# An encoder on one core: first column blocks side by side, a shared sine product, and the order of high and low weight products

## Chip, cores and metric

The kernel runs on one core of a Trainium2 chip. The metric is the device time of one execution in microseconds (us); lower is better. Each time is compared with runs of the kernel before on the same chip.

## The reference

A bidirectional encoder of two layers, for 256 positions of width 2048, all in float32. Cut to what matters:

```python
for i in range(2):
    hn = rms_norm(h, mix_norm[i])
    h = h + (mixer_a(hn, ...) if i % 2 == 0 else mixer_b(hn, ...))
    h = h + conv_ffn(rms_norm(h, ffn_norm[i]), w_up[i], conv_w[i], conv_b[i], w_down[i])
return rms_norm(h, final_norm)

def mixer_a(h, w_qkv, w_o, q_gain, k_gain):      # 16 query heads, 4 key/value heads of 128
    q, k, v = split(h @ w_qkv)                   # w_qkv: 2048 x 3072
    q, k = axial_rope(rms_norm(q, q_gain)), axial_rope(rms_norm(k, k_gain))
    return softmax(q @ k.T / sqrt(128)) @ v @ w_o

def mixer_b(h, w_qkv, w_o, rel_bias):            # 3 groups of 8 heads, dilations 1, 4, 16
    ...                                          # w_qkv: 2048 x 9216, w_o: 3072 x 2048

def conv_ffn(h, w_up, conv_w, conv_b, w_down):   # 2048 x 11264, 5632 x 2048
    gate, val = split(conv3(h @ w_up) + conv_b)
    return (silu(gate) * val) @ w_down
```

The rotary embedding multiplies each head by a cosine table and, with its quarters swapped, by a sine table, and adds the two.

## The kernel before

**High and low parts.** Every large product is made from two parts of each operand. A weight tile arrives as `raw` (float32), ScalarE copies it into `wh`, the rounded high part, and VectorE subtracts, `wl = raw - wh`. Activations are held in the same way, transposed, as `xh` and `xl` (or `ah` and `al` for the inner results). A product is then three matmuls: high by high, high activations by low weights, low activations by high weights. In each, the activation is the 128x128 stationary operand and the weights are the 128x512 moving operand.

**Feeds.** Weights are packed in blocks of 512 rows (a k group `kg`, four k tiles `kt` of 128) by 512 columns (a column block `n`). `feed` (L133) fetches one such 1 MB block by two DMAs on SP's queue into two `raw` tiles, rounds each (L163 on ScalarE, L164 on VectorE), and issues 24 matmuls into two accumulators `accs[m]`, one for each half `m` of the positions. For each `kt` and `m` they stand as three in a row:

```python
nc.tensor.matmul(accs[m], xh[:, c], wh[:, j, :], start=st, stop=False)    # L151
nc.tensor.matmul(accs[m], xh[:, c], wl[:, j, :], start=False, stop=False) # L152
nc.tensor.matmul(accs[m], xl[:, c], wh[:, j, :], start=False, stop=sp)    # L153
```

There are four `raw` tiles (`NRAW`) and four pairs `wh`, `wl` (`NHL`), each for half a feed. After every six matmuls `step` (L79) may take one step of a pending generator: the softmax, the transposes or the rounding of other heads are thus laid between the products. The order of instructions on each engine comes from a scheduler that follows the program order, with the rounding brought forward by `AHEAD` places.

**Who uses it.** `project` (L176) runs `feed` over all k groups of one column block; `project2` (L220) does two column blocks, with the last `late` groups of both at the end. They serve the two mixers' input and output projections and `w_down`. `w_up` goes through `feed_T` (L98), which has matmuls of its own (L125, L127), and the very last column block through `project_last`.

**The start.** `mixer_a` (L607) begins with `project2` on column blocks 4 and 5 (k and v). `hook` (L664) fetches, along the way, the transposed input `xT` in groups of four k tiles (`load_xT`, L634: DMA at L638, then high and low parts with the gain, L244 and L247), the input `h` itself (`load_x`, L659), and the rotary tables (`tables`, L618). The first two k groups of each block come in four pieces of 256 KB; with the first group, `xT` comes in pieces too. Order: three k groups of block 4, three of block 5, then the last group of 4 and of 5. Before any of it, `NWARM` = 11 matmuls on zeros run (L323). POOL's queue loads the identity `ident` (L51) and the taps of the convolution, `cr` (`load_taps`, L352: L356, L357), which TensorE later transposes (L364).

**Heads of mixer A.** `qk_post` (L679) takes a projected block: ScalarE scales it out of the accumulators into `stg` (L559), POOL makes the sine product `t` in four instructions (L694: two halves `m`, two `e`), VectorE the cosine product (L697), then their sum `ro` (L699). For q, `attend` then transposes `ro` on TensorE (L576).

**Mixer B** scales its probabilities on VectorE (L920) before TensorE transposes them (L922).

Of the kernel before, what the change touches and what calls it, by code (L numbers as in the profile page):

```python
# [7 lines left out]
F32 = mybir.dt.float32  # L8
# [16 lines left out]
NWARM = 11  # L25
# [3 lines left out]
def tile_encoder(ctx: ExitStack, tc: tile.TileContext, x, xT, w_a, w_ao, q_gain, k_gain, w_b, w_bo,  # L29
# [21 lines left out]
    nc.gpsimd.dma_start(ident, ident_c)  # L51
# [81 lines left out]
    def feed(accs, lhs, kg, wap, first, last, by_m=False, pieces=1, mid=None):  # L133
        raws, w = [], 2048 // pieces
        for i in range(max(pieces, 2)):
            if pieces < 4 or i % 2 == 0:
                raws.append(spool.tile([P, 2, 512], F32, tag="raw", name=nm("raw"), bufs=NRAW))
            w = min(w, 1024)
            r = raws[-1].rearrange("p a c -> p (a c)")
            k = i % 2 if pieces == 4 else 0  # L140
            nc.sync.dma_start(r[:, k * w:(k + 1) * w], wap[:, i * w:(i + 1) * w])
            if mid is not None:
                mid(i)

        def mms(order):
            for m, kt in order:
                (wh, wl), j = hls[kt // 2], kt % 2
                xh, xl = lhs[4 * kg + kt][:2]
                st, sp = first and kt == 0, last and kt == 3
                c = slice(m * P, (m + 1) * P)  # L150
                nc.tensor.matmul(accs[m], xh[:, c], wh[:, j, :], start=st, stop=False)  # L151
                nc.tensor.matmul(accs[m], xh[:, c], wl[:, j, :], start=False, stop=False)  # L152
                nc.tensor.matmul(accs[m], xl[:, c], wh[:, j, :], start=False, stop=sp)  # L153

        hls = []
        for s in range(2):
            wh = spool.tile([P, 2, 512], F32R, tag="wh", name=nm("wh"), bufs=NHL)
            wl = spool.tile([P, 2, 512], F32R, tag="wl", name=nm("wl"), bufs=NHL)
            r = raws[s]
            with tc.high_priority(offset=AHEAD):  # L160
                for i in range(max(pieces // 2, 1)):
                    c = slice(i, i + 1) if pieces == 4 else slice(0, 2)
                    nc.scalar.activation(wh[:, c], r[:, c], AF.Copy)  # L163
                    nc.vector.tensor_tensor(wl[:, c], r[:, c], wh[:, c].bitcast(F32), ALU.subtract)  # L164
            hls.append((wh, wl))
            if not by_m:
                for kt in (2 * s, 2 * s + 1):
                    mms([(m, kt) for m in range(2)])
                    step(kt % 2 == 0)
        if by_m:  # L170
            mms([(m, kt) for m in range(2) for kt in range(4)])
# [48 lines left out]
    def project2(w, n0, n1, lhs, kgs, late, first_done, hook=None):  # L220
        a0, a1 = new_acc(), new_acc()
        early = len(kgs) - late
        for k, part in enumerate((range(early), range(early, len(kgs)))):
            if k == 1:
                drain()
            for accs, n in ((a0, n0), (a1, n1)):
                for i in part:
                    kg = kgs[i]
                    mid = hook and hook(n == n0, kg)
                    feed(accs, lhs, kg, w[n, kg], i == 0, i == len(kgs) - 1,  # L230
                         pieces=4 if hook and i < 2 else 2 if hook else 1, mid=mid)
                if k == 1 and n == n0:
                    first_done(a0)
        return a1
# [117 lines left out]
    def load_taps(l):  # L352
        cr = spool.tile([P, 3, P], F32, tag="cr", name=nm("cr"), bufs=1)
# [253 lines left out]
    def mixer_a():  # L607
        with tc.tile_pool(name="apool", bufs=1) as ap:
# [25 lines left out]
            def load_xT(n):  # L634
# [10 lines left out]
                if n > 0:  # L645
                    load(0, 4)
                    for j in range(4):
                        prep(j)
                    return None
                load(0, 1)  # L650

                def mid(i):
                    if i < 3:
                        load(i + 1, i + 2)
                    prep(i)

                return mid
# [6 lines left out]
            def hook(first_block, kg):  # L664
                if first_block and kg < 3:
                    return load_xT(kg)
                elif first_block:
# [3 lines left out]
                elif kg == 0:  # L671
                    load_xT(3)
                elif kg == 1:
                    load_x(0)
                    tables()
                elif kg == 2:
                    load_x(1)

            def qk_post(accs, which, keep, scale=1.0):  # L679
# [10 lines left out]
                for m in range(2):  # L690
                    t5, s5 = (t[:, m, :].rearrange("p (a f e c) -> p a f e c", a=4, f=2, e=2) for t in (t2, s))
                    st5 = st[:, m, :].rearrange("p (f e c) -> p f e c", f=2, e=2)
                    for e in range(2):
                        nc.gpsimd.tensor_tensor(t5[:, :, :, e, :], s5[:, :, :, 1 - e, :],  # L694
# [111 lines left out]
    def mixer_b(hT, ss_in):  # L806
        with tc.tile_pool(name="bpool", bufs=1) as bp:
# [24 lines left out]
            cw, turn = load_taps(1)  # L832
# [216 lines left out]
```

## Time and profile before

| | us |
|---|---|
| median of 3 runs | 2287.27 (2287.05 to 2287.48) |
| the profiled execution | 2287.0 |
| its span, first to last instruction | 2284.9 |
| TensorE (PE) busy | 2273.9 |
| VectorE (DVE) busy | 1609.2 |
| ScalarE (ACT) busy | 1191.7 |
| GpSimd (POOL) busy | 188.6 |

The profiled execution's own time is its span and 2.1 us around it. In rows of the timeline the first number is the start, the second the duration, both in us from the span's start; an arrow in brackets names what ended the idle time before the instruction. The duration of a matmul is that of one pass through a pipeline; the next starts earlier. SP is the queue that issues most DMAs.

### The profile page before, as it was taken

What the parts mean: (1) busy time and instruction counts of PE and PEld (TensorE: products, weight loads), DVE (VectorE), ACT (ScalarE), POOL (GpSimd) and SP (SyncE); (2) the same over time, 40 slices, a digit from 0 to 9 for tenths busy, and PEclk for the clock granted to TensorE, in tenths of its full rate; (3) what the DMA queues carried; (4) which work ended last, traced back from release to release, by engine and by line L of the source; (5) the groups of instructions that cost most, each with busy time, mean ns of one, the idle gap of its engine ahead of it and who ended that gap; (6) DMA issues with size and microseconds to landing.
All of it is one profiled execution on the core that took longest, in us unless ns stands there. A gap on an engine that the chain in (4) does not pass through costs nothing.

```text
span 2284.9 us, 31058 instructions
## 1 busy us (share of the span) xinstructions
PE 2273.9 (100%) x11613; PEld 1943.2 (85%) x11613; DVE 1609.2 (70%) x2277; ACT 1191.7 (52%) x1737; POOL 188.6 (8%) x212
## 2 busy tenths in 40 slices
PE   9999999999999999999999999999999999999998
PEld 7888888888888888888888888888888888888887
DVE  6877877776457776878876876676777744677754
ACT  7565565554345554545454554445555533555543
POOL 2331000000000000010030003000000000000011
PEclk9999999999999999999999999999999999999999
DMA  8545656666655666576655555566565666556564
GB/s 301 167 130 165 202 186 186 187 194 198 194 186 185 194 190 197 184 222 203 188 180 182 176 189 169 179 201 201 188 194 187 191 196 193 189 189 193 185 198 153
DMA packets 256727, 433.43 MB, mean 190 GB/s; under 512 B 13752, under 2 KB 194744, under 8 KB 256448
## 3 DMA queue, kind: packets, MB, share of 16 engines
q1 hardware_dynamic: 254768, 425.91, 58.4%
q0 software_dynamic: 1520, 5.25, 1.1%
q8 instruction: 91, 1.49, 0.3%
q14 instruction: 60, 0.49, 0.1%
q10 hardware_dynamic: 288, 0.30, 0.0%
HBM read 429.20 MB, written 2.20 MB: 189 GB/s over the span
## 4 chain that ended last, share of the span: by engine, by line
PE 98%; DVE 1%; issue 1%; ACT 0%; POOL 0%; DMA 0%; SPq 0%; POOLq 0%; DVEq 0%; ACTq 0%
PE acc L127 28%; PE acc L152 17%; PE acc L153 17%; PE acc L151 17%; PE acc L125 15%; PE ps L255 1%; PE ps L254 0%; PE ps L256 0%; PE ps L762 0%; PE ps L252 0%; PE ps L938 0%; DVE wl L164 0%; DVE tT L281 0%; DMA raw<-in_w_a_dram 0%; POOL t L694 0%
## 5 line engine op out<-in xcount | busy, mean ns | idle before, releaser
L164 DVE TENSOR_TENSOR wl<-raw,wh 128x1024 fp32r<-128x1024 f32 (+1 forms) x452 | 548.7, 1217 | 307.2 <-ACT wh L163 303.8
L163 ACT ACTIVATE wh<-raw 128x1024 fp32r<-128x1024 f32 (+1 forms) x452 | 470.2, 1044 | 500.6 <-PE acc L153 412.4
L127 PE MATMUL acc<-xh,wh 128*128 128x512 f32 x2816 | 658.2, 390 | 0.0
L127 PEld LDWEIGHTS acc<-xh,wh 128*128 128x128 f32 x2816 | 522.4, 188 | 105.2 <-DVE v L400 0.5
L112 DVE TENSOR_TENSOR wl<-raw,wh 128x1024 fp32r<-128x1024 f32 x352 | 416.7, 1222 | 88.0 <-ACT wh L111 79.6
L111 ACT ACTIVATE wh<-raw 128x1024 fp32r<-128x1024 f32 x352 | 362.6, 1053 | 67.9 <-ACT v L399 30.2
L151 PE MATMUL acc<-wh,ah 128*128 128x512 f32 x1008 | 392.8, 390 | 0.0
L153 PE MATMUL acc<-wh,al 128*128 128x512 f32 x1008 | 392.3, 389 | 0.0
L152 PE MATMUL acc<-wl,ah 128*128 128x512 f32 x1008 | 392.3, 389 | 0.0
L125 PEld LDWEIGHTS acc<-xh,wl 128*128 128x128 f32 x2816 | 350.4, 192 | 7.5
L125 PE MATMUL acc<-xh,wl 128*128 128x256 f32 x2816 | 352.7, 283 | 0.0
L151 PE MATMUL acc<-wh,xh 128*128 128x512 f32 x768 | 302.3, 394 | 1.0 <-ACT wh L163 1.0
L152 PE MATMUL acc<-wl,xh 128*128 128x512 f32 x768 | 299.7, 390 | 0.2 <-DVE wl L164 0.2
L153 PE MATMUL acc<-wh,xh 128*128 128x512 f32 x768 | 299.8, 390 | 0.0
L153 PEld LDWEIGHTS acc<-wh,al 128*128 128x128 f32 x1008 | 189.2, 188 | 39.6
L151 PEld LDWEIGHTS acc<-wh,ah 128*128 128x128 f32 x1008 | 189.2, 188 | 38.8
L152 PEld LDWEIGHTS acc<-wl,ah 128*128 128x128 f32 x1008 | 189.2, 188 | 38.7
L153 PEld LDWEIGHTS acc<-wh,xh 128*128 128x128 f32 x768 | 144.1, 188 | 30.6
L151 PEld LDWEIGHTS acc<-wh,xh 128*128 128x128 f32 x768 | 144.4, 188 | 29.2 <-ACT wh L163 1.4
L152 PEld LDWEIGHTS acc<-wl,xh 128*128 128x128 f32 x768 | 144.3, 188 | 28.7 <-DVE wl L164 0.9
L419 POOL TENSOR_TENSOR cv<-cg,cv 128x512 f32<-128x512 f32 x44 | 59.9, 1361 | 1164.5 <-DVE cv L411 1145.3
L240 ACT ACTIVATE ah<-cv 128x256 fp32r<-128x256 f32 x88 | 31.9, 410 | 169.0 <-POOL cv L419 169.0
(178 smaller groups left out, 1484.1 us busy)
## 6 DMA issues: line engine op xcount, KB each, us to landing
raw<-in_w_up_dram SPq DMA_DIRECT2D x352, 512.0 KB, 4.7
raw<-in_w_down_dram SPq DMA_DIRECT2D x176, 512.0 KB, 3.8
raw<-in_w_b_dram SPq DMA_DIRECT2D x144, 512.0 KB, 3.9
raw<-in_w_bo_dram SPq DMA_DIRECT2D x48, 512.0 KB, 3.7
raw<-in_w_a_dram SPq DMA_DIRECT2D x40, 512.0 KB, 4.4
raw<-in_w_ao_dram SPq DMA_DIRECT2D x32, 512.0 KB, 3.7
raw<-in_w_a_dram SPq DMA_DIRECT2D x16, 256.0 KB, 5.7
h<-in_x_dram SPq DMA_DIRECT2D x4, 512.0 KB, 7.7
```

Source lines behind the costliest of these rows:

```text
L111: nc.scalar.activation(wh, rk, AF.Copy)
L112: nc.vector.tensor_tensor(wl, rk, wh.bitcast(F32), ALU.subtract)
L125: nc.tensor.matmul(acc[j][:, :NT], w2[1][:, kt, c], x[0], start=st, stop=sp)
L127: nc.tensor.matmul(acc[j], w2[0][:, kt, c], x[2], start=st, stop=sp)
L151: nc.tensor.matmul(accs[m], xh[:, c], wh[:, j, :], start=st, stop=False)
L152: nc.tensor.matmul(accs[m], xh[:, c], wl[:, j, :], start=False, stop=False)
L153: nc.tensor.matmul(accs[m], xl[:, c], wh[:, j, :], start=False, stop=sp)
L163: nc.scalar.activation(wh[:, c], r[:, c], AF.Copy)
L164: nc.vector.tensor_tensor(wl[:, c], r[:, c], wh[:, c].bitcast(F32), ALU.subtract)
L240: nc.scalar.activation(hi, src, AF.Copy)
L255: nc.tensor.matmul(o, lh[ls], rl[rs], start=False, stop=False)
L419: nc.gpsimd.tensor_tensor(cv, cg, cv, ALU.mult)
```

## The change

- `NWARM` goes from 11 to 9.
- `ident` is loaded by SP, behind the weights of the second k group, instead of by POOL at the start.
- The taps `cr` get no tile of their own but the place of another one: in mixer A that of `qTl`, which first holds the second `xT` group, so that the load waits until that group has been used; in mixer B that of `pTl`.
- A new `feed_first` runs the first k group of column blocks 4 and 5 side by side: for each k tile, the products of both blocks. Its first two k tiles come in single pieces, the other two as a pair. `xT` comes in pieces 1, 1, 2. There, in the first two k tiles, `m` = 0 takes low activations before low weights.
- After that, `project2` at the start goes group by group through both blocks, and `hook` places the loads of `h`, `ident` and the tables anew.
- `feed` no longer splits its DMAs into smaller pieces, and its new `mm_half` issues, for each half feed (two k tiles), eight matmuls with high weights and then four with low ones.
- For the first q alone (`shared`), VectorE makes the two sine products of `m` = 1, POOL those of `m` = 0.

```diff
-NWARM = 11
+NWARM = 9
...
-    nc.gpsimd.dma_start(ident, ident_c)
...
+    def round_raw(hl, r, c):
+        nc.scalar.activation(hl[0][:, c], r[:, c], AF.Copy)
+        nc.vector.tensor_tensor(hl[1][:, c], r[:, c], hl[0][:, c].bitcast(F32), ALU.subtract)
+
+    def mm_kt(accs, lhs, kg, hls, m, kt, first, last, skewed=False):
+        (wh, wl), j = hls[kt // 2], kt % 2
+        xh, xl = lhs[4 * kg + kt][:2]
+        c = slice(m * P, (m + 1) * P)
+        terms = [(xh, wh), (xl, wh), (xh, wl)] if skewed else [(xh, wh), (xh, wl), (xl, wh)]
+        for i, (xx, ww) in enumerate(terms):
+            nc.tensor.matmul(accs[m], xx[:, c], ww[:, j, :], start=first and kt == 0 and i == 0,
+                             stop=last and kt == 3 and i == 2)
+
+    HALF = [(0, 0, 0, 0), (0, 0, 1, 0), (0, 1, 0, 0), (0, 1, 1, 0), (1, 0, 0, 0), (1, 1, 0, 0),
+            (1, 0, 1, 0), (1, 1, 1, 0), (0, 0, 0, 1), (1, 0, 0, 1), (0, 1, 0, 1), (1, 1, 0, 1)]
+
+    def mm_half(accs, lhs, kg, hl, s, first, last):
+        for i, (j, m, lx, lw) in enumerate(HALF):
+            rest = [o[1] for o in HALF[i + 1:]]
+            nc.tensor.matmul(accs[m], lhs[4 * kg + 2 * s + j][lx][:, m * P:(m + 1) * P], hl[lw][:, j, :],
+                             start=first and s == 0 and i == 2 * m, stop=last and s == 1 and m not in rest)
+            if i % 6 == 5:
+                step(i == 5)
+
+    def feed_first(accs2, lhs, waps, load, prep):
...
+        for k0, k1 in ((0, 1), (1, 2), (2, 4)):
+            load(k0, k1)
+            for b in range(2):
+                fetch(b, k0, k1)
+        for kt in range(4):
+            prep(kt)
+            for b in range(2):
+                round_raw(hls[b][kt // 2], raws[b][kt // 2], slice(kt % 2, kt % 2 + 1))
+            for b in range(2):
+                for m in range(2):
+                    mm_kt(accs2[b], lhs, 0, hls[b], m, kt, True, False, kt < 2 and m == 0)
...
     def project2(w, n0, n1, lhs, kgs, late, first_done, hook=None):
...
+        if hook:
+            feed_first((a0, a1), lhs, [w[n, kgs[0]] for n in (n0, n1)], *hook(0, 0))
+            order = [(i, b) for i in range(1, early) for b in range(2)]
+        else:
+            order = [(i, b) for b in range(2) for i in range(early)]
+        order += [(i, b) for b in range(2) for i in range(early, len(kgs))]
...
-    def load_taps(l):
-        cr = spool.tile([P, 3, P], F32, tag="cr", name=nm("cr"), bufs=1)
+    def load_taps(l, t):
+        cr = t[:, :3 * P].rearrange("p (a c) -> p a c", a=3)
...
-            def hook(first_block, kg):
+            def hook(i, b, behind=False):
+                if (i, b) == (0, 0):
+                    return load_xT(0)
+                if not behind:
+                    if b == 0 and i < 3:
+                        load_xT(i)
+                elif (i, b) == (1, 1):
+                    nc.sync.dma_start(ident, ident_c)
+                    load_x(0)
+                    load_x(1)
+                elif (i, b) == (2, 1):
+                    load_xT(3)
                     load_x(2)
+                elif (i, b) == (3, 0):
+                    tables()
                     load_x(3)
                     rstd.append(finish_rstd(ss_in))
...
+                    eng = nc.vector if shared and m else nc.gpsimd
                     for e in range(2):
-                        nc.gpsimd.tensor_tensor(t5[:, :, :, e, :], s5[:, :, :, 1 - e, :],
+                        eng.tensor_tensor(t5[:, :, :, e, :], s5[:, :, :, 1 - e, :],
...
-            cw, turn = load_taps(0)
+            cw, turn = load_taps(0, ap.tile([P, 4 * NT], F32, tag="qTl", name="cr0"))
...
-                yield from qk_post(accs, "q", keep, SCALE)
+                yield from qk_post(accs, "q", keep, SCALE, g == 0)
...
-            cw, turn = load_taps(1)
+            cw, turn = load_taps(1, bp.tile([P, 2 * NT], F32, tag="pTl", name="cr1", bufs=2))
```

More of the change, by code (lines that the diff above doesn't have):

```diff
@@ L131, in feed_T, with half_raw @@
                     step()
[L133 to L153, printed above, removed]
+    def half_raw():
+        return spool.tile([P, 2, 512], F32, tag="raw", name=nm("raw"), bufs=NRAW)
@@ L648, in load_xT @@
                         prep(j)
[L649 to L657, printed above, removed]
+                return load, prep
             def load_x(n):
```

66 lines of the change are left out of this document (33 added, 33 removed).

## Prediction

> **What bounds the kernel now.** I read the page first: the span, the busy shares, then the chain that ended last.
>
> ```profile
> span 2284.9 us, 31058 instructions
> PE 2273.9 (100%) x11613; PEld 1943.2 (85%) x11613; DVE 1609.2 (70%) x2277; ACT 1191.7 (52%) x1737; POOL 188.6 (8%) x212
> PE 98%; DVE 1%; issue 1%; ACT 0%; POOL 0%; DMA 0%; SPq 0%; POOLq 0%; DVEq 0%; ACTq 0%
> ```
>
> TensorE is busy throughout, and 98% of the chain is its own matmuls. The change takes no matmul away but two warm-ups, so it can win only where the stream of products halts or runs slower than its pace. The pace comes from TensorE's timeline, in an undisturbed stretch:
>
> ```profile
> 44.67 0.39 PE L151 MATMUL acc<-wh,xh 128*128 128x512 f32 x1
> 46.03 0.39 PE L151 MATMUL acc<-wh,xh 128*128 128x512 f32 x1
> ```
>
> These rows are six products apart: 1.36/6 = 0.2267 us each (the 0.39 is a pipelined latency). I went through TensorE's timeline for starts further apart than this. Halts that the edits can touch stand in three places: the first 19 us, the first q's transposes, and two transposes of mixer B.
>
> **The change part by part.**
>
> *Start of mixer A.* TensorE's timeline, then the groups by line from 5.5 to 18.8 us:
>
> ```profile
> 4.78 0.85 PE L323 MATMUL ps<-warm 128*128 128x512 f32 x3
> 5.47 0.39 PE L151 MATMUL acc<-wh,xh 128*128 128x512 f32 x1
> 5.82 0.50 PE L152 MATMUL acc<-wl,xh 128*128 128x512 f32 x1
> 6.85 0.40 PE L153 MATMUL acc<-wh,xh 128*128 128x512 f32 x1
> 8.25 0.50 PE L151 MATMUL acc<-wh,xh 128*128 128x512 f32 x1 [1.00 <-ACT wh L163]
> 8.97 0.50 PE L152 MATMUL acc<-wl,xh 128*128 128x512 f32 x1 [0.23 <-DVE wl L164]
> 13.01 0.27 PE L364 MATMUL ps<-ident,cr 128*128 128x128 f32 x1
> 18.82 0.39 PE L151 MATMUL acc<-wh,xh 128*128 128x512 f32 x1
> ...
> L152 PE MATMUL acc<-wl,xh 128*128 128x512 f32 x16 | 6.6, 410 | 0.2 <-DVE wl L164 0.2
> L151 PE MATMUL acc<-wh,xh 128*128 128x512 f32 x16 | 6.3, 403 | 1.0 <-ACT wh L163 1.0
> L153 PE MATMUL acc<-wh,xh 128*128 128x512 f32 x16 | 6.3, 393 | 0.0
> ```
>
> The last three warm-ups start at 4.78 and the first product at 5.47, so a late warm-up costs (5.47 - 4.78)/3 = 0.23 us; two fewer bring the first product to 5.47 - 0.46 = 5.01. From 5.47 to 18.82 stand 48 products: 48 x 0.2267 = 10.88 of 13.35 us, so 2.47 us were lost. The largest pieces: 8.25 - 6.85 - 0.23 = 1.17 us for the second k tile's high weights, 8.97 - 8.25 - 0.23 = 0.49 for its low ones, 0.12 for low weights at 5.82. The three tap transposes lie in this stretch too. 24 products stand before 13.01; the other 24 take from there to 18.82, 5.81 us instead of 5.44, so these transposes and their wake cost 0.37. They move to after product 96 and after product 252 of the built order, and are paid there: neutral. What can go is 2.47 - 0.37 = 2.10 us.
>
> Does it go? The weights' path is DMA, ScalarE, VectorE:
>
> ```profile
> 4.41 0.63 ACT L163 ACTIVATE wh<-raw 128x512 fp32r<-128x512 f32 x1 [0.64 <-DMA raw<-in_w_a_dram]
> 5.08 0.69 DVE L164 TENSOR_TENSOR wl<-raw,wh 128x512 fp32r<-128x512 f32 x1 [0.79 <-ACT wh L163]
> 6.92 0.51 ACT L244 ACTIVATE xh<-xt,gain 128x256 fp32r<-128x256 f32 x1 [1.87 <-DMA xt<-in_xT_dram]
> ...
> 4.00:7.00 3.00, 3.00 (x12) 2.03 (x11) 0.98 (x2) 0.72 (x2) 0.00 (x0) 1.00 0.89 244
> 8.00:12.00 4.00, 3.53 (x14) 2.68 (x15) 3.19 (x6) 3.17 (x8) 0.00 (x0) 1.00 1.05 399
> ...
> ident<-in_ident_dram POOLq DMA_DIRECT2D x1, 64.0 KB, 4.5
> cr<-in_conv_dram POOLq DMA_DIRECT2D x2, 128.0 KB, 5.5
> ```
>
> ScalarE sat 1.87 us for the second xT piece. The table of stretches (last column GB/s) shows the DMA engines at 244 GB/s from 4 to 7 us and 399 from 8 to 12; in the slow stretch POOL's loads of `ident` and the taps `cr` share them. The change takes both away: `ident` goes onto SP's queue behind the second k group's weights, `cr` waits on POOL until the second xT group is read.
>
> The other half is demand. Today a k tile feeds six products, 1.36 us, with 384 KB. Side by side it feeds twelve, 2.72 us, with 640 KB: 235 GB/s instead of 282, below even the slow rate. I walk through at the slow rate. The first block's piece is there at 4.4 as now, high at 5.04, low at 5.77. TensorE starts at 5.05, its second product takes the low part of x instead of the low weights, the third waits until 5.8: 0.3 us lost. The second block's piece (256 KB, 1.05 us) lands at 5.45, is high by 6.1 and low by 6.8; TensorE comes to it at 6.7 and wants low weights at 7.2. The next xT piece lands at 6.0, the two weight pieces at 7.0 and 8.1; wanted, in high form, at 8.1 and 9.5: 0.63 us of rounding fits. So two k tiles hold even at 244; for the last two, with 512 KB per block, 399 is the nearer row, as POOL issues nothing then. Bounds for the loss that stays: 0 (pieces some tenths earlier) and 2.0 (244 to the end: the first block's last pair lands at 11.2 and is high at 11.9 where TensorE is ready at 10.8, then 0.6 more for the second block). I take 0.2. The start gives 0.46 + 2.10 - 0.2 = 2.35 us.
>
> Work moved on SP: the x loads follow the second and third groups, `rope` and the gains the fourth's first. They serve the k evacuation, which cannot start before 168 products, about 43 us; SP's queue reaches the last x load at about 24 us (the fourth group's buffers come free with the third's rounding, and that waits for the second group's first 72 products, 5 + 16.3 = 21 us), so some 19 us cover it. POOL's tap loads wait until the second xT group is scaled, by the walk above about 14 us; only the rotary tables stand behind them, and TensorE wants taps and `ident` after product 96, at 5 + 22 = 27 us. Were they later, each us would cost one.
>
> *First q.* TensorE, POOL and VectorE around it, and the nearest VectorE row for a sine product (two SBUF inputs, one broadcast):
>
> ```profile
> 81.17 0.39 PE L153 MATMUL acc<-wh,xh 128*128 128x512 f32 x1
> 82.14 1.10 PE L576 MATMUL ps<-ident,ro 128*128 128x128 f32 x8 [0.59 <-DVE ro L699]
> ...
> 74.36 5.51 POOL L694 TENSOR_TENSOR t<-stg,st_q 128x256 f32<-128x256 f32 x4 [16.67 <-ACT stg L559]
> ...
> 73.97 1.22 DVE L164 TENSOR_TENSOR wl<-raw,wh 128x1024 fp32r<-128x1024 f32 x1
> 75.47 1.41 DVE L697 TENSOR_TENSOR ro<-stg,ct_q 128x1024 f32<-128x1024 f32 x1 [0.28 <-ACT stg L559]
> 77.93 3.02 DVE L164 TENSOR_TENSOR wl<-raw,wh 128x1024 fp32r<-128x1024 f32 x2
> 80.88 1.21 DVE L699 TENSOR_TENSOR ro<-ro,t 128x1024 f32<-128x1024 f32 x1
> ...
> L900 DVE TENSOR_TENSOR pr<-pr,e 128x256 f32<-128x256 f32 x16 | 7.7, 522 | 0.0
> ```
>
> TensorE is ready at 81.17 + 0.23 = 81.40 and starts at 82.14: 0.74 us lost. POOL's four products end at 79.87, but the sum `ro` begins only at 80.88, behind two roundings of low weights. In the built order two sine products (2 x 0.52 = 1.04 us) come ahead of the cosine product and only one rounding stands ahead of the sum. From 75.2: 1.04 + 1.41 + 1.2 + 1.22 + 1.21 gives 81.3, just in time (this is in the times of before; the start shifts all alike). Gain 0.7; bounds 0.74, and the loss of the port rival below. The delayed rounding feeds products 3 us or more later, as four rounded halves are held.
>
> The Trainium skill, "SBUF — State Buffer", section "SBUF: two separate sides", speaks against this part: VectorE with two SBUF inputs and GpSimd share a port pair as an exclusive lock, so one blocks for the whole of the other's instruction. This trace bears that out in part only, by the 3.02 above for two roundings of 1.22. By the rule the part would lose time, not gain it.
>
> *Eight high, then four low, everywhere.* How many products that touches, from the page's groups:
>
> ```profile
> L151 PE MATMUL acc<-wh,ah 128*128 128x512 f32 x1008 | 392.8, 390 | 0.0
> ...
> L151 PE MATMUL acc<-wh,xh 128*128 128x512 f32 x768 | 302.3, 394 | 1.0 <-ACT wh L163 1.0
> ```
>
> 3 x (1008 + 768) - 48 = 5280 products outside the first k group are reordered, none is added, and in the built order every other matmul keeps its place among them, bar the taps and the two below. Low weights are wanted 1.6 us later after the high ones, and high buffers come free four products (0.9 us) earlier: relief for ScalarE and VectorE, but nothing waits there now. The pace itself need not change:
>
> ```profile
> 293.96 5.15 PE L127 MATMUL acc<-xh,wh 128*128 128x512 f32 x22
> ```
>
> In this stretch of the gated MLP 22 products change accumulator and weights at every step; from first start to last start they take (5.15 - 0.39)/21 = 0.2267 each, the same pace. So I cost the order at 0, with plus or minus 1 us for the slower products after small matmuls, which it might lengthen or shorten.
>
> *Mixer B.* Two halts remain:
>
> ```profile
> 1159.20 0.39 PE L153 MATMUL acc<-wh,xh 128*128 128x512 f32 x1
> 1159.67 0.63 PE L922 MATMUL ps<-ident,pr 128*128 128x128 f32 x4
> ...
> 1370.81 0.39 PE L153 MATMUL acc<-wh,xh 128*128 128x512 f32 x1
> 1371.29 0.63 PE L922 MATMUL ps<-ident,pr 128*128 128x128 f32 x4
> ```
>
> 0.47 - 0.23 = 0.24 and 0.25 us, for VectorE's scaled probabilities. In the built order both transposes stand six products (1.4 us) later, while the scaling keeps its place: both halts go, 0.45 us. Their result is wanted 12 products (2.7 us) on, for which 1160.0 to 1161.7, some 1.7 us, is what the split takes now.
>
> **Sum.** 2.35 + 0.7 + 0 + 0.45 = 3.5 us off the profiled execution's 2287.0, 2283.5; the median of 2287.27 is 0.27 above it, so I predict 2283.8, 0.15% less. A measurement of this kernel can tell about 0.2% from no change, 4.6 us; the halts named add up to 0.46 + 2.10 + 0.74 + 0.49 = 3.8, so this change alone hardly reaches that.
>
> **Rivals.**
> - *The start stays short of data.* If 244 GB/s lasts through the fourth k tile, the start loses 2.0 instead of 0.2: 2285.6. For it: both blocks' pieces come in the first microseconds. Against: the row of 399 once POOL's loads are through. Chance 0.11.
> - *The sine products block each other.* The edit then does not do what it says: VectorE's two wait for POOL's two, which end at 74.36 + 5.51/2 = 77.1 instead of being started at 75.2: 1.9 us later than above, the sum ends at 83.2, and 1.8 us are lost where 0.74 are now. 2283.8 + 0.7 + 1.1 = 2285.6. Against: the cosine product started at 75.47, amid POOL's, and took 1.41 only. Chance 0.08. The rule of the Trainium skill above would make this of it.
> - *The new order slows the pace (slower).* Place: 5280 products. Price: 5.3 us per ns. From 0.65 ns on (3.5/5280) the change loses; at 1 ns 2289.1, at 2 ns 2294.4. For it: so many products that the smallest effect counts. Against: the 22 products of line 127, in yet another order, at the same pace within 0.5 ns (the row's 0.01 us over 21). Chance 0.07.
> - *The order also shortens the wake of small matmuls*, beyond the 1 us allowed: 2282 or less. Nothing speaks for it. Chance 0.04.
>
> **Numbers.** The forecast has 0.70. Its own bounds run from 2283.8 - 0.3 - 1.0 = 2282.5 to about 2285; the first two rivals, both at 2285.6 with half a us of slack, are taken in: 2282.4 to 2286.2. Left out are the slow pace, the larger gain and some of the forecast's own edges, about 0.15. Faster by over 0.2% (below 2282.7): 0.06, the last rival and the forecast's lower edge. Slower by over 0.2%: 0.05, the pace rival from 1.5 ns on and what goes unseen. Within: 0.89.
>
> **What would show it.** Right: first product near 5.05, no gap above 0.3 us until 16 us, 48 products by 16.1; the first q's transposes with no wait for `ro`, mixer B's with none for `pr`; products of the new helper 0.2267 apart; the end of the last product 3 to 4 us earlier. Wrong: ScalarE waiting for `raw` around 9 to 13 us; VectorE's sine products starting only after POOL's; a spacing above 0.2267 in stretches with nothing between; a halt at the tap transposes after product 96.

## The result, and the profile after

| | before | after |
|---|---|---|
| median, us (lowest to highest) | 2287.15 (2286.45 to 2287.98) | 2290.89 (2288.84 to 2291.75) |
| span of the profiled execution, us | 2284.9 | 2289.2 |

The ratio after to before is 1.0015, 95% interval 1.0009 to 1.0021. Predicted were 3.5 us less, 2283.8; it became 3.7 us more, outside the range of 2282.4 to 2286.2. The page, with the span, two busy shares and the chain that ended last:

```profile
span 2289.2 us, 31074 instructions
PE 2275.4 (99%) x11611; PEld 1945.1 (85%) x11611; DVE 1609.9 (70%) x2275; ACT 1192.1 (52%) x1733; POOL 184.4 (8%) x209
PE 96%; DVE 1%; DMA 1%; issue 1%; ACT 0%; SPq 0%; POOL 0%; DVEq 0%; POOLq 0%
```

These lines hardly differ from before: 70% of VectorE and 98 or 96% of the chain are averages over 2.3 ms. The loss is in TensorE's timeline (start, duration, how many; the last start of a group of n is (n - 1) x 0.2267 behind its first):

```profile
1.46 4.21 PE L359 MATMUL ps<-warm 128*128 128x512 f32 x9 [1.46 <-DVE warm L356]
5.46 1.00 PE L148 MATMUL acc<-wh,xh 128*128 128x512 f32 x2
...
16.91 1.98 PE L157 MATMUL acc<-wh,xh 128*128 128x512 f32 x8
...
27.80 0.27 PE L400 MATMUL ps<-ident,cr 128*128 128x128 f32 x1
28.78 1.43 PE L157 MATMUL acc<-wh,xh 128*128 128x512 f32 x5 [0.70 <-ACT wh L139]
...
79.98 1.07 PE L157 MATMUL acc<-wl,xh 128*128 128x512 f32 x4
84.70 1.93 PE L612 MATMUL ps<-ident,ro 128*128 128x128 f32 x8 [3.65 <-DVE ro L731]
86.28 2.97 PE L157 MATMUL acc<-wh,xh 128*128 128x512 f32 x8
...
90.00 0.28 PE L290 MATMUL ps<-kTh,qTh 128*128 128x256 f32 x1
```

The row that stands there in the kernel before:

```profile
85.83 0.28 PE L254 MATMUL ps<-kTh,qTh 128*128 128x256 f32 x1
```

I call halt the time beyond 0.23 us between two starts.

- The first product starts at 5.46, where before had 5.47: in these two profiles the nine warm-ups took as long as eleven. From there to the 49th product it is 16.91 - 5.46 = 11.45 us, 13.35 before: 1.9 us won. The 2.1 - 0.2 predicted sets aside the 0.37 us of the tap transposes, which have left this stretch too, so that 2.27 were due in it. Of the 11.45 - 10.88 = 0.57 us still lost, 0.39 lie in the first two products, which take from 5.46 to 6.30.
- Behind the tap transpose at 27.80, TensorE waits for high weights, 0.9 us that before did not have.
- At the first q, the last product ahead starts at 79.98 + 0.68 = 80.66, the transposes at 84.70: a halt of 3.8 us, where before had 0.74 and the prediction none. The eight transposes and the twelve products behind them then take from 84.70 to 90.00, 5.30 us; before they took from 82.14 to 85.83, 3.69 us: 1.6 us more.

The table of stretches shows why these are slow (the last columns: granted clock PEclk, DMA share, GB/s):

```profile
80.00:84.00 4.00, 1.04 (x5) 0.54 (x3) 4.00 (x5) 1.99 (x3) 0.00 (x0) 1.00 0.46 147
84.00:86.00 2.00, 1.30 (x7) 1.30 (x8) 2.00 (x4) 0.19 (x1) 1.20 (x1) 0.69 0.67 233
86.00:88.00 2.00, 2.00 (x7) 1.71 (x7) 2.00 (x3) 1.01 (x2) 2.00 (x1) 0.50 0.59 213
88.00:90.00 2.00, 2.00 (x10) 1.57 (x10) 0.19 (x1) 0.71 (x1) 0.48 (x1) 0.95 0.72 221
```

After its pause TensorE works at half its clock (0.50) until about 88 us. VectorE (third pair) is busy for the whole of 80 to 88. Its timeline up to the sum `ro`:

```profile
73.16 0.53 DVE L401 COPY cw<-ps 128x352 f32<-128x352 f32 x1
73.71 2.36 DVE L140 TENSOR_TENSOR wl<-raw,wh 128x1024 fp32r<-128x1024 f32 x2
75.99 1.76 DVE L277 TENSOR_TENSOR kTl<-tT,kTh 128x1024 fp32r<-128x1024 f32 x1
77.68 1.76 DVE L140 TENSOR_TENSOR wl<-raw,wh 128x1024 fp32r<-128x1024 f32 x1
79.36 0.75 DVE L726 TENSOR_TENSOR t<-stg,st_q 128x256 f32<-128x256 f32 x2
80.03 1.21 DVE L729 TENSOR_TENSOR ro<-stg,ct_q 128x1024 f32<-128x1024 f32 x1
81.17 1.21 DVE L732 TENSOR_REDUCE ssq<-sq 128x8 f32<-128x1024 f32 x1
82.30 1.21 DVE L140 TENSOR_TENSOR wl<-raw,wh 128x1024 fp32r<-128x1024 f32 x1
83.43 1.21 DVE L731 TENSOR_TENSOR ro<-ro,t 128x1024 f32<-128x1024 f32 x1
```

No row has an idle time in brackets: nothing is waited for, there is simply more work queued than time. It had been so since 46.7 us. What was late at the beginning is seen on ScalarE, first after, then before:

```profile
41.60 0.64 ACT L312 ACTIVATE junk<-h 128x512 f32<-128x512 f32 x1 [3.23 <-DMA h<-in_x_dram]
...
42.99 1.04 ACT L139 ACTIVATE wh<-raw 128x1024 fp32r<-128x1024 f32 x1
45.04 0.69 ACT L595 ACTIVATE stg<-acc,rstd 128x512 f32<-128x512 f32 x1 [1.00 <-PE acc L157]
45.62 1.05 ACT L139 ACTIVATE wh<-raw 128x1024 fp32r<-128x1024 f32 x1
46.57 0.68 ACT L595 ACTIVATE stg<-acc,rstd 128x512 f32<-128x512 f32 x1
...
47.71 1.06 ACT L139 ACTIVATE wh<-raw 128x1024 fp32r<-128x1024 f32 x1
```

```profile
43.52 1.06 ACT L163 ACTIVATE wh<-raw 128x1024 fp32r<-128x1024 f32 x1 [1.66 <-PE acc L153]
45.62 1.31 ACT L559 ACTIVATE stg<-acc,rstd 128x512 f32<-128x512 f32 x2 [1.04 <-PE acc L153]
```

Count the weights in halves of feeds, twelve products each, from 0. Half 16 is the first of the q blocks; TensorE reaches it at 51.48 before and at 50.67 after. Its rounding is the row at 43.52 before, ahead of the first evacuation of k (`stg`, 45.62), and the row at 47.71 after, behind both. ScalarE first stood 3.23 us for the last part of `x` with roundings queued behind. The lead shrank from 8 us to 3, and the low roundings so put off lie in VectorE's queue ahead of k's chain and of the first q's.

In mixer B the two halts did not go but grew, from 0.24 and 0.25 to 0.43 each:

```profile
1162.56 1.23 DVE L140 TENSOR_TENSOR wl<-raw,wh 128x1024 fp32r<-128x1024 f32 x1 [0.79 <-ACT wh L139]
1163.71 0.18 DVE L918 TENSOR_TENSOR lsum<-lsum,e 128x24 f32<-128x24 f32 x1
...
1165.27 0.63 PE L954 MATMUL ps<-ident,pr 128*128 128x128 f32 x4 [0.26 <-DVE pr L952]
```

A low rounding that waits for its high half, 0.79 + 1.15 us, now stands amid the short chain that leads to the scaling, and eats the 1.4 us by which the transposes were moved.

### The profile page after: what moved, and what is told of

Read it like the earlier page. It is cut to its first block, busy times and chain, and to the rows that moved or that the text cites. A ratio compares the mean times of both kernels' runs of the same rounds, so it can differ in the third digit from the quotient of the medians.

```text
span 2289.2 us, 31074 instructions
## 1 busy us (share of the span) xinstructions
PE 2275.4 (99%) x11611; PEld 1945.1 (85%) x11611; DVE 1609.9 (70%) x2275; ACT 1192.1 (52%) x1733; POOL 184.4 (8%) x209
## 4 chain that ended last, share of the span: by engine, by line
PE 96%; DVE 1%; DMA 1%; issue 1%; ACT 0%; SPq 0%; POOL 0%; DVEq 0%; POOLq 0%
PE acc L157 50%; PE acc L126 28%; PE acc L124 15%; DVE wl L140 1%; PE ps L291 0%; PE ps L290 0%; PE ps L292 0%; DMA xt<-in_xT_dram 0%; PE ps L794 0%; PE ps L288 0%; PE ps L970 0%; DMA raw<-in_w_a_dram 0%; DVE tT L317 0%; PE ps L612 0%; PE ps L954 0%
## 5 line engine op out<-in xcount | busy, mean ns | idle before, releaser
L157 PE MATMUL acc<-wh,xh 128*128 128x512 f32 x1504 | 380.1, 393 | 0.7 <-ACT wh L139 0.7
L157 PE MATMUL acc<-wh,ah 128*128 128x512 f32 x1008 | 351.8, 390 | 0.0
L157 PE MATMUL acc<-wh,al 128*128 128x512 f32 x1008 | 351.6, 389 | 0.0
L157 PEld LDWEIGHTS acc<-wh,xh 128*128 128x128 f32 x1504 | 277.5, 188 | 55.6 <-ACT wh L139 1.1
L157 PE MATMUL acc<-wl,ah 128*128 128x512 f32 x1008 | 269.5, 389 | 0.0
L157 PE MATMUL acc<-wl,xh 128*128 128x512 f32 x752 | 201.3, 389 | 0.0
L436 DVE TENSOR_TENSOR v<-acc,v 128x256 f32<-128x256 f32 x176 | 73.8, 420 | 50.2 <-ACT v L435 50.2
L277 DVE TENSOR_TENSOR al<-cv,ah 128x256 fp32r<-128x256 f32 x88 | 33.5, 422 | 81.9 <-ACT ah L276 81.9
```

The lines of the kernel that those rows point to most:

```text
L157: nc.tensor.matmul(accs[m], lhs[4 * kg + 2 * s + j][lx][:, m * P:(m + 1) * P], hl[lw][:, j, :], start=first and s == 0 and i == 2 * m, sto ...
L277: nc.vector.tensor_tensor(lo, src, hi.bitcast(F32), ALU.subtract)
L436: nc.vector.tensor_tensor(v[:, j], acc[j][:, :NT], v[:, j], ALU.add)
```

## The experiments

The three parts are called start (side by side, with its loads and nine warm-ups), order (eight high, four low) and sharing (of the sine). All medians stand beside runs of the kernel before on the same chip in the same session (2287.15 to 2287.43); each halt is that of one profile.

| | halt at the first q | median | ratio, 95% interval |
|---|---|---|---|
| before | 0.74 | 2287.2 to 2287.4 | |
| sharing alone | 0.16 | 2286.99 | 0.9998 (0.9989 to 1.0007) |
| order alone | 2.05 | 2289.38 | 1.0010 (1.0001 to 1.0018) |
| order and sharing | 2.45 | 2290.59 | 1.0014 (1.0005 to 1.0022) |
| start alone | 2.04 | 2288.68 | 1.0007 (0.9998 to 1.0016) |
| start and order | 3.71 | 2290.97 | 1.0016 (1.0007 to 1.0025) |
| all three (after) | 3.82 | 2290.89 | 1.0015 (1.0009 to 1.0021) |
| start, x rearranged | 0.82 | 2286.63 | 0.9996 (0.9987 to 1.0005) |
| the same with sharing | 0.35 | 2285.71 | 0.9993 (0.9984 to 1.0002) |
| all three, x rearranged | 2.43 | 2288.50 | 1.0007 (0.9998 to 1.0016) |

*Is it the sharing, or the start?* My first theory was that the new start takes the rounding's lead; its rival, that the sine products on VectorE make the halt. After, without sharing:

```diff
-                yield from qk_post(accs, "q", keep, SCALE, g == 0)
+                yield from qk_post(accs, "q", keep, SCALE)
```

> The kernel after, but all four sine products of the first q on POOL again. After lost 3.82 us before the first q's transposes, and about 2.1 us in slow products behind them. Theory A (the new start costs ScalarE and VectorE two halves of rounding lead: the rounding of the half that TensorE starts at 50.67 begins at 47.7, 3.0 us ahead, where before it began 8 us ahead; VectorE is then busy without a gap from 46.7 to 87 us and the first q's chain comes late whoever forms the sine): the halt stays, 3 us or more (VectorE is spared 0.67 us, but POOL's four products of 1.27 us end only near 81 us), time 2290 to 2291.5. Theory B (the two sine products on VectorE, and their cover on its port, make the halt): the halt falls below 1 us, the slow products go with it, time 2285 to 2286.5.

Measured 2290.97, halt 3.71: the sharing is not the cause. POOL's four products ended at 81.94, 1.6 us ahead of the sum at 83.54, which stood behind VectorE's own queue. With the old start and the other two parts:

```diff
 NWARM = 11
...
+            if not by_m and pieces < 4:
+                mm_half(accs, lhs, kg, hls[s], s, first, last)
...
+                    eng = nc.vector if shared and m else nc.gpsimd
```

> The kernel before (old start: one column block after the other, eleven warm-ups, identity and taps loaded first), with the other two parts of the change: the new product order wherever the weights come in whole halves, and the first q's sine products shared. Theory A (the new start is what makes the first q late): rounding keeps its lead of about 8 us at 50 us, the halt before the first q's transposes is below 0.7 us, and the time is 2286.2 to 2287.5. Theory B (the shared sine products): the halt is 3 us or more and the time above 2290.

Measured 2290.59, the time that the rival forecast, with a halt of 2.45, between the two forecasts. The theory that the start alone is guilty falls. The third part alone, on the kernel before:

```diff
+            if not by_m and pieces < 4:
+                mm_half(accs, lhs, kg, hls[s], s, first, last)
```

> The kernel before with the new product order alone (wherever the weights come in whole halves). If the order costs nothing, as predicted: the spacing stays 0.2267 us and the time lies within 1 us of before, 2286.2 to 2288.1. If the order slows the pace by 0.5 ns per product: 2.6 us more, about 2289.8. The two halts of mixer B, which grew from 0.24 and 0.25 to 0.43 us in after, should show here as well if the order makes them (a rounding of low weights then stands between the scores and the scaling), 0.4 us in all.

The first two groups of the first two blocks come in quarter pieces and keep the old order here; 5232 products are reordered. Measured 2289.38, halt 2.05, and 0.43 twice in mixer B. The pace kept its 0.2267 us; the order costs 2.0 us without slowing one product. Where it does is seen in the timelines of ScalarE, VectorE and TensorE of this kernel:

```profile
40.52 1.06 ACT L174 ACTIVATE wh<-raw 128x1024 fp32r<-128x1024 f32 x1 [0.18 <-DVE wl L175]
45.97 0.69 ACT L572 ACTIVATE stg<-acc,rstd 128x512 f32<-128x512 f32 x1 [4.39 <-PE acc L139]
46.55 1.05 ACT L174 ACTIVATE wh<-raw 128x1024 fp32r<-128x1024 f32 x1
...
47.64 1.62 DVE L175 TENSOR_TENSOR wl<-raw,wh 128x1024 fp32r<-128x1024 f32 x1 [4.80 <-ACT wh L174]
...
83.58 1.09 PE L589 MATMUL ps<-ident,ro 128*128 128x128 f32 x8 [1.89 <-DVE ro L712]
```

The rounding of half 16 (46.55) has changed places with the first evacuation of k (45.97). ScalarE idles 4.39 us, VectorE 4.80, and the whole chain to the first q starts late. I revised the theory: both the order and the start put this rounding behind k's evacuation, and the two add.

*Does the pause itself slow the products behind it?* After, with idle products (whose result is unused) in the pause:

```diff
+                if g == 0:
+                    o = ps_tile()
+                    for _ in range(14):
+                        nc.tensor.matmul(o, hT[0][2][:, :P], hT[0][2], start=True, stop=True)
```

> The kernel after, with 14 idle products of 512 columns (14 x 0.2267 = 3.2 us; their result is used by nothing) on TensorE right ahead of the first q's transposes, where it stood still for 3.82 us. If the slow products behind the halt (transposes 1.93 us in place of 1.10, then products 0.43 us apart until 87.9) come from the pause itself, because TensorE's clock falls in it: they go, and the time falls by about 2.1 us to 2288.8, though 3.2 us of work are added. If they have another cause (late weights, say), the time stays at 2290.9 or rises.

```profile
80.37 3.35 PE L766 MATMUL ps<-xh 128*128 128x512 f32 x14
83.55 1.03 PE L612 MATMUL ps<-ident,ro 128*128 128x128 f32 x8
84.34 2.09 PE L157 MATMUL acc<-wh,xh 128*128 128x512 f32 x8
...
81.81 1.21 DVE L731 TENSOR_TENSOR ro<-ro,t 128x1024 f32<-128x1024 f32 x1
```

Measured 2288.10, 2.8 us less with 3.2 us of work more. Without the pause the products behind it are not slow, and some 1.6 us of the gain is that. The rest is not the pause's: the transposes start 1.15 us sooner than in after (83.55 against 84.70). This profile came to product 97 0.5 us sooner, and the edit changed VectorE's order too: the rounding that stands ahead of the sum in after (82.30) now comes behind it.

*Which of the reordered products?* The new order only in the third and fourth groups of the first two blocks, and its complement, both on the kernel before:

```diff
+            if not by_m and pieces == 2:    # the one; the complement: pieces < 2
+                mm_half(accs, lhs, kg, hls[s], s, first, last)
```

> The kernel before with the new product order only in the third and fourth weight groups of the first two column blocks (96 products); all other products in the old order. With the new order everywhere but the start, TensorE waited 2.05 us for the first q and 0.43 twice in mixer B, and the time rose by 2.0 us. In that kernel's built order ScalarE's rounding of half 16 (the first of the q columns) stands behind the first evacuation of k instead of ahead of it: VectorE then idled 4.80 us up to 47.64, where before it idled 1.49 and 1.20, and all of its work up to the first q is that much later. Theory A (that exchange in ScalarE's queue is the whole loss at the first q): here the exchange is there too, so the halt is again about 2 us and the time 2288.2 to 2289.5; mixer B's halts stay at 0.24 and 0.25. Theory B (the loss comes from the many products of the later blocks, whose low weights are released later): the halt is about 0.75 us and the time is that of before, 2287.4.

> The kernel before with the new product order everywhere but in the first two column blocks: the complement of the kernel with the order in those blocks alone. In its built order ScalarE's rounding of half 16 stands ahead of the evacuation of k, as before; one low rounding has moved ahead of the first q's cosine product, but as many stand ahead of its sum as before. Theory A (the exchange in the first two blocks makes the halt at the first q): the halt is as before, 0.7 us, the time 2287.4 to 2288 with mixer B's 0.35 us. Theory B (the later blocks make it): halt about 2 us, time 2289 or more.

Measured 2288.76 with a halt of 1.88, and 2287.64 (ratio 1.0002, 0.9993 to 1.0011) with 0.93. By the halts it is as the revised theory has it: 96 products make the halt, and the other 5136 cost next to nothing, 0.35 us of it in mixer B. The times alone do not show it, as the interval of the first (ratio 1.0006, 0.9997 to 1.0015) takes in 1 too.

*Can the first q come later?* After, with one more step ahead of the transposes:

```diff
-                yield
+                for _ in range(2 if g == 0 else 1):
+                    yield
```

> The kernel after, with the first q's transposes (and all attention work behind them) one step of 12 products, 2.72 us, later in TensorE's order. If the 3.82 us halt and the slow products behind it are the loss: the halt falls to about 1.1 us, the clock does not fall, and 2.7 + 2.1 us come back: 2286 to 2286.8, below the kernel before. If the later attention work only moves the halt on (the split of q, the scores' maxima), the time stays above 2289.

Measured 2290.72: a miss. The halt fell to 1.1 us and the clock stayed up, but three new halts of 1.40, 1.41 and 1.75 us came at the last head of each of the first three q blocks. VectorE's timeline at the first of them, then TensorE's:

```profile
101.38 1.47 DVE L729 TENSOR_TENSOR ro<-stg,ct_q 128x1024 f32<-128x1024 f32 x1
...
104.51 1.40 DVE L140 TENSOR_TENSOR wl<-raw,wh 128x1024 fp32r<-128x1024 f32 x1
105.84 0.15 DVE L785 RECIPROCAL l<-l 128x2 f32<-128x2 f32 x1
...
107.26 0.66 PE L795 MATMUL ps<-ident,pr 128*128 128x128 f32 x4 [1.24 <-POOL pr L786]
```

The next q's cosine product and a rounding now stand ahead of this head's reciprocal; without the edit the reciprocal came first (106.59, the cosine product at 107.96).

*What of the start costs lead?* After, with the loads of `x` rearranged and their squares later in ScalarE's queue (from here on: x rearranged; the third group of `xT` is loaded one feed earlier as well), then the start alone with both orders of `x`:

```diff
-                sumsq_cols(ss_in, n, junk)
...
                 elif (i, b) == (1, 1):
                     nc.sync.dma_start(ident, ident_c)
+                    tables()
                     load_x(0)
+                elif (i, b) == (2, 0):
                     load_x(1)
                 elif (i, b) == (2, 1):
                     load_xT(3)
                     load_x(2)
+                    load_x(3)
+                    sumsq_cols(ss_in, 0, junk)
+                    sumsq_cols(ss_in, 1, junk)
                 elif (i, b) == (3, 0):
-                    tables()
-                    load_x(3)
+                    sumsq_cols(ss_in, 2, junk)
+                    sumsq_cols(ss_in, 3, junk)
                     rstd.append(finish_rstd(ss_in))
```

> The kernel after, with the loads of x and of the third xT group moved on SP's queue and the squares of x later on ScalarE's: the third xT group is loaded one feed earlier, the rotary tables behind the identity, the fourth part of x beside the third, and the squares of the first two parts come behind the third group's feeds, so that ScalarE does not stand waiting for x (3.23 us at 41.60 and 0.65 and 0.44 earlier) with roundings queued behind. Theory A (the new start costs rounding lead through these waits): the halt of 0.9 us behind the tap transpose at 27.8 goes, the halt at the first q falls from 3.8 to about 2 us, what the new order alone left, and the time falls to 2286.5 to 2288.5. Theory B (the lead is lost elsewhere): the halt stays at 3.5 us or more, the time at 2289.5 or more.

> The kernel after without its other two parts: first two column blocks side by side, nine warm-ups, the loads moved; old product order in all whole groups, all sine products of the first q on POOL. In its built order ScalarE's rounding of half 16 stands behind the second evacuation of k (before: ahead of the first; order alone: behind the first), and the squares of x stand ahead of roundings as in after. Theory A (what the new start takes from the rounding's lead makes the first q late, as does the new order; the two add): halt 1.5 to 2.5 us at the first q, 0.9 us at product 96, mixer B as before; with the 1.9 us won by product 48 the time is 2286.5 to 2288.5. Theory B (only the order does harm): halt 0.7 us, time 2285 to 2286.

> The side-by-side start alone (old product order, sine on POOL), with the loads and squares of x rearranged so that no rounding waits behind them. In its built order ScalarE's rounding of half 16 stands ahead of k's evacuation, as before. Theory A: no halt at product 96, about 0.7 us at the first q, 0.5 us in mixer B as before; what is left is the start's own gain of 1 to 2 us, time 2285 to 2286.3, below the kernel before. Theory B (the side-by-side start itself, by its weights' order, delays k's chain): halt 2 us or more, time 2287.5 or more.

Measured 2288.50 (halt 2.43, none behind the tap transpose, one of 0.44 at 41.9), 2288.68 (2.04, and 0.44 there) and 2286.63 (0.82, and 0.41 there). Rearranging `x` took 2.4 us off with the new order and 2.05 without. With the rounding of half 16 back ahead of k's evacuation (44.15 against 45.43) the side-by-side start comes out 0.8 us below before in the median, but its interval takes in 1, so a gain is not shown. Nor does the halt behind the tap transpose show what the rearranging did: kernels that start just as after does have it at 1.16 us (sine on POOL), 0.18 (one step later) and not at all (idle products) in their one profile each.

*The sharing by itself, and the warm-ups.* One edit each, to before and to after:

```diff
+                    eng = nc.vector if shared and m else nc.gpsimd
```

> The kernel before with one edit: the second row half of the first q's sine products on VectorE. Its built order has the two sine products and the cosine product, then two low roundings, then the sum; the reduction of the squares, which stood ahead of the sum, now stands behind it. By the prediction's step (0.7 us gained, as the sum no longer comes behind POOL and the reduction): halt 0 to 0.2 us at the first q, time 2286.5 to 2286.9. If VectorE's products wait for POOL's, or each slows the other: VectorE's two take 1.5 us or more in place of 0.75, the halt is 1 us or more and the time above 2287.5.

```diff
-NWARM = 9
+NWARM = 11
```

> The kernel after with eleven warm-ups instead of nine. If each warm-up saved brings the first product forward (0.43 us each while the clock is at half, which in nine of the ten profiles so far is the case for the last ones): the time rises by 0.4 to 0.9 us to 2291.3 to 2291.8. If the clock opens after so much work rather than at a time, two more warm-ups cost what two slow products cost now, and the time stays within 0.3 us of 2290.9.

Sharing alone: 2286.99, and the halt is gone, as predicted for this part; the time is 0.44 us below before, with an interval that takes in 1. VectorE's row for its two products, then TensorE's:

```profile
75.93 1.48 DVE L695 TENSOR_TENSOR t<-stg,st_q 128x256 f32<-128x256 f32 x2 [0.28 <-ACT stg L559]
...
81.62 0.39 PE L153 MATMUL acc<-wh,xh 128*128 128x512 f32 x1
82.01 1.09 PE L576 MATMUL ps<-ident,ro 128*128 128x128 f32 x8
```

They took 1.48 us beside POOL's, 0.75 where POOL had ended (79.36 above). With eleven warm-ups: 2290.47, 0.4 us below nine, not above; the intervals of the two overlap. Two warm-ups are worth nothing that shows. In the profiles the moment at which the pace changes from some 0.43 to 0.23 us per product moves from one execution to the next: with eleven warm-ups the first product starts at 5.47 (before), at 5.58 (here) and at 6.31 or 6.32 (the five other kernels with the start of before), with nine between 4.98 and 5.58.

*All together.* Start with `x` rearranged and sharing, with the new order in the second and third groups of the first blocks (first), nowhere (second), and everywhere but in their last group (third):

```diff
+            feed(accs, lhs, kg, w[n, kg], i == 0, i == len(kgs) - 1, new=hook and i < 3)
```

> Side-by-side start with the rearranged x loads and squares, shared sine products, new product order only in the second and third weight groups of the first two blocks, old order elsewhere. In its built order the rounding of half 16 stands ahead of k's evacuation, and the reduction of the first q's squares behind its sum. Theory A (the exchange in ScalarE's queue is the whole loss; the parts gain without it): halt at the first q 0.2 us at most, no wait for low weights at product 96 (0.44 us in the same start with the old order), 0.5 us in mixer B as before; time 2285.0 to 2286.2. Theory B (the parts cost elsewhere too): 2286.6 or more, no better than the start alone.

> The same with the old product order in all whole groups. Against the kernel with the rearranged start alone (halt 0.82 us, 2286.63) it adds only the shared sine products: halt 0.2 us, time 2286.0 by the 0.59 us that the halt shrank in the kernel before with sharing alone; 2286.6 if sharing gains nothing here.

> The kernel after with the rearranged x loads and squares, and the old product order only in the last weight group of the first two blocks (96 products); the new order stays in all others, and sharing too. In its built order the rounding of half 16 is ahead of k's evacuation again. Theory A (these 96 products make the exchange): the halt falls from 2.43 us, with the order new there as well, to about 0.9 us (the reduction and one rounding still stand ahead of the sum), the clock does not fall in any run, time 2286.3 to 2287 with mixer B's 0.35 us. Theory B (the new order of the later blocks matters too): halt 1.5 us or more, time 2287.5 or more.

Measured 2287.18 (1.0000, 0.9991 to 1.0009), 2285.71 and 2288.43 (1.0004, 0.9995 to 1.0013). The second is the fastest of all, 5.2 us below after and 1.7 below before in the median, though its interval against before still takes in 1. The other two missed. The third's halt at the first q, 1.52, and its time are on the rival's side; and both had a halt of 1.70 us that no theory named. In the third the rounding of half 16 does stand ahead of k's evacuation (44.97 against 46.12), but only after ScalarE has waited 3.25 us for its weights. VectorE's and TensorE's timelines of the first:

```profile
40.81 0.52 DVE L402 COPY cw<-ps 128x352 f32<-128x352 f32 x1 [3.48 <-PE ps L401]
...
42.80 0.51 PE L158 MATMUL acc<-wl,xh 128*128 128x512 f32 x1 [1.53 <-DVE wl L140]
```

VectorE, in order, stands 3.48 us before its copy of the taps until TensorE reaches their transposes at 40.53; the low rounding behind the copy then keeps TensorE waiting. So theory A, that the exchange is the whole of the loss, is not shown for the mixed orders: each built order brings waits of its own.

## Why the prediction was wrong, point by point

- **Start.** The data part was right: 1.9 us by product 48, and 0.18 us lost beside the slow first two products, where 0.2 was forecast. (The demand of 235 GB/s counts 1000 bytes to the KB; with 1024 it is 241, still below 244.) The rival of a start short of data did not come. The warm-up term failed: I priced the two that went by the 0.23 us of the last ones before, but all nine went at some 0.44 each (4.00 us in all), and the first product came at 5.46, not 5.01. The column PEclk reads 1.00 in this stretch, so it does not show why.
- **"Work moved on SP"** failed twice. SP's queue was to reach the last load of `x` at about 24 us, with some 19 us of cover to k's evacuation. It came to it at 32.94, and ScalarE first read that part at 41.60, 3.4 us ahead of the evacuation at 45.04:

```profile
32.94 0.55 SPq L688 DMA_DIRECT2D h<-in_x_dram x1
```

  And I asked only whether `x` would be there for that evacuation. Its squares are ScalarE instructions, in order, and the roundings behind them had no such cover: 3.23 us at 41.60. The 0.9 us at product 96 is of the same kind, ScalarE's high weights come late, but differs from profile to profile, as said above.
- **First q.** The working stood on "the start shifts all alike". That is the step that failed: k's chain and the roundings did not shift with TensorE. VectorE's cosine product came at 80.03 instead of some 76, and 3.8 us were lost where none were forecast. Sharing itself does what was said where all else stays, 0.74 to 0.16: there the built order puts the reduction of the squares behind the sum. With the new order it stays ahead, and sharing lengthens the halt, 2.05 to 2.45: VectorE's two products take 1.85 us there, and the wait for POOL that they spare was 0.62. The rival that the sine products block each other was not the cause.
- **"Eight high, then four low" at 0** was right on pace and wrong on time. I had written "relief for ScalarE and VectorE, but nothing waits there now", and took every other matmul's unchanged place in TensorE's order for the whole effect. What moved was the order on ScalarE and VectorE. The rival that the order loses was right in sign, 2.0 us, by another mechanism: one exchange, not 5280 slower products.
- **Mixer B.** "The scaling keeps its place" was wrong: a rounding moved ahead of it. Forecast 0.45 less, measured 0.37 more.
- **What the halt costs.** The prediction let a microsecond of halt cost one. The 3.8 us cost 1.6 more in slow products, and 2.7 in the profile with the sine on POOL, where the granted clock stayed at 0.50 until 90.5 us. The Trainium skill, "TensorE: Matmul & The Clock Gate", Part 1 on the clock gate, has this: after an idle window of about 3.4 us TensorE runs at half rate. The trace agrees here, 1.00 to 0.50 after 3.8 us.
- **The range** ended at 2286.2, as only the pace rival could lose. Two parts that left TensorE's order as it was met in ScalarE's queue, and no rival looked there.

In the profiled executions, after stands 0.5 us ahead at the last product before the first q's transposes (80.66 against 81.17): 1.9 won by product 49, 1.0 lost at the first tap transpose and 0.4 around the other two, which I had put down as neutral. At the first q it loses 4.7 us (3.1 of halt, 1.6 of clock), in mixer B 0.4. Less the 0.5 ahead that is 4.6 us lost, where the span grew by 4.3; the other 0.3 was not traced. Why the scheduler makes the exchange was not tried and stays open.

## What to carry to other kernels

When an edit changes what frees a buffer or where a load is issued, compare the built order of every engine, not only the one that bounds: look for work with a short lead (here the rounding of half 16) that changes places with work that must wait. Ask of each moved DMA which in-order instruction reads it and what is queued behind that. A halt of TensorE has to be priced with the slow clock that may follow.

## What the runs showed of the hardware that I had not expected

The clock did not fall at one length of halt. In one profile each, it stayed up after 1.88, 2.05 and 2.43 us (order in the first blocks, order alone, all three with `x` rearranged) and fell after 2.04 and 2.45 (start alone, order with sharing). The table of stretches of the start alone, then of order with sharing:

```profile
84.00:86.00 2.00, 2.00 (x11) 1.80 (x10) 2.00 (x3) 1.20 (x2) 2.00 (x1) 0.59 0.80 242
```

```profile
86.00:88.00 2.00, 2.00 (x6) 1.52 (x5) 1.63 (x3) 0.00 (x0) 1.93 (x1) 0.50 0.73 240
```

The same page of the Trainium skill says that the window runs free, so that the moment of the change varies; that would fit, but its 3.4 us of idleness is more than these halts. The measurement decides: 2 us can be enough.

VectorE's subtractions, 1.22 us elsewhere, took 1.76 in after (the low rounding at 77.68 above, and the split of k at 75.99), beside POOL's two products of 1.27 each:

```profile
75.82 2.53 POOL L726 TENSOR_TENSOR t<-stg,st_q 128x256 f32<-128x256 f32 x2 [16.66 <-ACT stg L595]
```

They were each 0.54 us longer. The Trainium skill's rule of an exclusive lock ("SBUF — State Buffer", "SBUF: two separate sides"), by which one would wait for the other's whole instruction, is borne out in part: not 1.27.
